# Two re-dated steps in a planned decoder block: VectorE's part of the RNN batches, and the last Strassen product

## The chip, the core and the metric

The kernel runs on one core of a Trainium2 chip. The metric is device microseconds of one launch, from the chip's own clock. Five engines share the work: TensorE (PE in the profile, with its weight loads as PEld), VectorE (DVE), ScalarE (ACT), GpSimd (POOL), and SyncE (SP), which only issues DMAs here.

## The reference, cut to what matters

One decoder block for 512 tokens of width 1024, in float32:

```python
xn   = rms_norm(h, g_mix) * (1 + sc1) + sh1
proj = xn @ w_in + b_in                    # q k v qi ki wi xr yr gate_a gate_b
attn = dsa_attention(q, k, v, qi, ki, wi)  # top-128 keys by an index score, softmax over those
xr   = causal_dwconv(xr)                   # width 4
a    = exp(log_a);  mult = sqrt(-expm1(2 * log_a))
h_r  = scan(a, xr * sigmoid(i) * mult)     # h[s] = a[s] * h[s-1] + u[s]
rnn  = h_r * gelu(yr)
merged = sigmoid(gate_a) * (attn @ w_o_attn) + sigmoid(gate_b) * (rnn @ w_o_rnn)
h    = h + ga1 * (merged @ w_out)
up   = causal_dwconv(xn2 @ w_up)           # width 3, 2 x 2816 columns
h    = h + ga2 * ((silu(gte) * val) @ w_down)
out  = rms_norm(h, g_final)
```

The change touches the order of two things: the scan and the two products around it (`u = xr*i*mult`, `h`, `h*gelu(yr)`), and the end of `act @ w_down`.

## The kernel before, in words

**Arithmetic.** Every float32 product is done as three float32r matmuls (`mm3`): each operand is split into a high part (a copy on ScalarE) and a low part (a subtraction on VectorE, line 470), and PE computes high*high + low*high + high*low. So each weight tile costs VectorE a subtraction before PE can use it. Everything lies in tiles of 128 partitions x 512 columns (`t`, 75 of them); raw weights land in three large buffers (`W`), split weights of projections in six (`w`).

**The planner.** The program is not written in issue order. Each step is recorded with its engine or engines, a cost in us from a formula, what it reads and writes, and optionally a due time; `Plan.order` then simulates the engines and emits the steps in the order in which it would have run them. A step's rank is its due time: the least of `P.fix` (main matmuls, which follow a nominal TensorE clock `clock[0]` that advances 0.227 us for each 512-column matmul), `P.soft`, and what its readers' ranks leave it. An engine takes, among the steps that can start within 0.12 us of the earliest, the one with the lowest rank. A step that needs a new buffer may not start earlier than its rank less a horizon (`P.hor`, normally `HORIZON`). On the chip every engine runs its own list in that order, and a step whose operand is late holds up all that stand behind it on its engine. Most constants in capitals (`ISTEP`, `IW`, `ASTEP`, `AW`, `RB`, `SOON`, `DOT1`, `LATER`, ...) are such due times or lower bounds.

**Stages on PE.** Seven projection tiles accumulate while the first weights arrive; then projection tiles of 24 matmuls each (`proj`); among them the RNN gates, the index scores, attention rows 0 to 3 (`attn_probs`, `attn_out`); the gates `gb`, `ga`; the projections `wr` (of the RNN) and `wa` (of attention); `w_out`; and the FFN.

**The RNN batches.** `rnn_batch` runs for heads 0 to 3 behind tile (yr, 3) and for heads 4 to 7 behind tile (yr, 7). `at(us)` dates a step at `base + us`. All four heads share the dates, so that ScalarE does each function for four tiles in one table phase: square root at `RB[3]` and gelu at `RB[4]`. Before the change VectorE's `u*m` and scan inherit `RB[3]`, and `y*h` inherits `RB[4]`. Behind (yr, 7) come the tiles (q, 1) to (q, 3), whose evacuation (`evac_stack`) ends in a VectorE step on line 475; attention row 0 reads them.

**The FFN's down projection.** `up(n)` makes 44 tiles: `proj`, a convolution (ScalarE, then two steps on line 475), silu and a product for every second one, which gives `acts[f]`, f from 0 to 21. For f up to 15 the down projection is done by Strassen's seven products in two slices (f 0 to 7 and f 8 to 15). `product(m, first, last)` prepares four pairs of operands on VectorE and runs 24 matmuls; `SPREAD` says behind which up tile each runs, `ORDER` which product it is. The remaining f, 16 to 21, are the tail: each output row block of 128 tokens (`ROWS` gives the order 2, 3, 0, 1) and half of the columns takes six `mm3`, then `total` is added, and the final norm and store follow.

Of the kernel before, what the change touches and what calls it, by code (L numbers as in the profile page):

```python
# [14 lines left out]
ALU = mybir.AluOpType  # L15
# [4 lines left out]
TT = S // 128  # L20
D_FF = 2816
FT = D_FF // 128
# [19 lines left out]
SLOTS = {"W": 3, "w": 6, "t": 75, "b": 8}  # L42
SHAPES = {"W": [128, 2048], "w": [128, 1024], "t": [128, 512], "b": [128, 512]}
INFLATE = 1.03
HORIZON = 26
EARLY = 3
PAIRS = 8
ORDER = [[4, 3, 0, 2, 1, 5, 6], [0, 1, 2, 3, 4, 5, 6]]
ROWS = [2, 3, 0, 1]
SLICES = [(0, 4), (4, 8)]  # L50
SPREAD = [[17, 19, 21, 23, 25, 27, 29], [32, 34, 36, 37, 39, 41, 42]]
OUTS = [("wr", (0, 1, 2, 3)), ("wa", (0, 1)), ("wr", (4, 5)), ("wa", (2, 3, 4, 5, 6, 7)), ("wr", (6, 7))]
ADA0 = 28
COLD = 8.0
RBIAS = [14.0, 46.0, 48.0]
WARM = 12
DOT1 = 13.24
SECOND = -23.6
LATER = 13.94
CLOCK = 9.79  # L60
RB = [3.28, 6.04, 7.96, 11.0, 13.85, 0.61]
SOON = [20.91, 19.0, 21.69, 11.19]
ISTEP = {1: 14.0, 2: 38.5, 3: 93.3}
IW = {1: 18, 2: 49.4, 3: 51.9}
ASTEP = {0: 76, 1: 99.0, 2: 126, 3: 145}
AW = [8.6, 6.1, 18.7, 30.4]
BUMP = [0.01, 0.81]


def tile_columns(kind, j):  # L70
# [83 lines left out]
def pass_us(n):  # L154
    return max(0.109, 0.0133 + n / 2400)
# [21 lines left out]
class Plan:  # L177
# [20 lines left out]

    def op(self, engs, reads, writes, emit, func=None, hold=(), n=1, tag="", follow=None):
        o = Op()  # L200
        o.engs, o.emit, o.func = engs, emit, func
        o.n, o.tag = n, tag
        o.shares = self.shares_port(engs, reads, writes, tag)
        o.soft, o.hor, o.after = self.soft, self.hor, self.after
        o.idx, o.fixed, o.succ = len(self.ops), self.fix, []
        deps, bufs = {follow} - {None}, []
        o.weak = set()
        for is_w, vs in ((False, reads), (True, writes)):
            for v in vs:
                if v is None or not isinstance(v, (Buf, View)):  # L210
                    continue
                v = vw(v)
                b = v.buf
                for box, w, p in b.users:
                    if (w or is_w) and overlap(box, v.bx):
                        deps.add(p)
        for is_w, vs in ((False, reads), (True, writes)):
            for v in vs:
                if v is None or not isinstance(v, (Buf, View)):
                    continue  # L220
                v = vw(v)
                v.buf.users.append((v.bx, is_w, o))
                if v.buf not in bufs:
                    bufs.append(v.buf)
        bufs += [b for b in hold if b not in bufs]
        deps.discard(o)
        for b in bufs:
            if b.first is None:
                b.first = o
            elif b.kind in SLOTS and b.first not in deps:  # L230
                o.weak.add(b.first)
        deps.discard(o)
        o.weak -= deps
        deps |= o.weak
        o.deps, o.bufs = deps, bufs
        for p in deps:
            p.succ.append(o)
        self.ops.append(o)
        return o
# [160 lines left out]
def block_kernel(ctx: ExitStack, tc: tile.TileContext, x, cols, wada1, wada2, win0, win, wgate,  # L400
# [10 lines left out]
    P = Plan()  # L411
# [6 lines left out]
    def t2(dt=F32, shape=(128, 512), name="t"):  # L418
        return buf("t", shape, dt, name, 10)

    def bank(reserve=0):
        return buf("b", (128, 512), F32, "ps", reserve)
# [28 lines left out]
    def act(dst, src, func, bias=0.0, scale=1.0, accum=None, hold=()):  # L451
        n = width(src)
        cost = max(0.2, 0.04 + 0.00094 * n) + 0.093 * sum(isinstance(v, (Buf, View)) for v in (bias, scale, accum))
        kw = {}

        def emit(e):
            if isinstance(bias, (Buf, View)) or bias:
                kw["bias"] = real(bias)
            if isinstance(scale, (Buf, View)) or scale != 1.0:
                kw["scale"] = real(scale)  # L460
            if accum is not None:
                kw["accum_out"] = real(accum)
            nc.scalar.activation(real(dst), real(src), func, **kw)  # L463
        P.op({"act": cost}, [src, bias, scale], [dst, accum], emit, func=func.name, hold=hold, n=1 + (accum is not None), tag="act")

    def tt(dst, a, b, op, engs=("dve",)):
        n = max(width(a), width(b))
        c = {"dve": 0.07 + 0.00104 * n, "pool": 0.05 + 0.0026 * n}
        P.op({e: c[e] for e in engs}, [a, b], [dst],
             lambda e: ENG[e].tensor_tensor(real(dst), real(a), real(b), op=op), tag="tt")  # L470
# [66 lines left out]
    def mm3(ps, wh, wl, xh, xl, first, last):  # L537
        mm([(ps, wh, xh, first, False), (ps, wh, xl, False, False), (ps, wl, xh, False, last)])
# [14 lines left out]

    clock = [CLOCK]

    def planned(us):
        P.fix = clock[0]
        clock[0] += us
# [26 lines left out]
    for h in range(2):  # L585
        ps = bank()
# [82 lines left out]
    for kt in range(KT):  # L669
# [26 lines left out]
        cuts = ((0, 2), (2, 4)) if kt == 0 else ((0, 4),)  # L696
        xn.append(modulate(xs, kt, modc[:, 8 + kt:9 + kt], modc[:, kt:kt + 1], cuts))
        for a, b in cuts:
            m = slice(128 * a, 128 * b)
            for n in range(len(G0)):  # L700
                c = slice(n % 4 * 128, n % 4 * 128 + 128)
# [118 lines left out]
    def rnn_batch(js):  # L820
        base = clock[0] + RB[0]

        def at(us):
            P.soft, P.hor = base + us, 1.0
        g = {}
        at(0.0)
        for j in js:
            xc = R[j]
            hi, lo = t2(F32R, name="xch"), t2(F32R, name="xcl")
            split(hi, lo, xc)  # L830
            whi, wlo = wg[j // 2]
            for e, b in ((0, "b_rg"), (1, "b_ig")):
                p = bank(2)
                c = slice(e * 128, (e + 1) * 128)
                mm3(p, whi[:, j % 2, c], wlo[:, j % 2, c], hi, lo, True, True)
                g[j, e] = t2(name="rg")
                act(g[j, e], p, AF.Sigmoid, bias=col(b, j))
            clock[0] += RB[5]
        am = {}
        for j in js:  # L840
            at(RB[1])
            r, u, xc = g[j, 0], g[j, 1], R[j]
            tt(u, u, xc, ALU.mult, ("dve", "pool"))
            t, a, m = t2(name="t"), t2(name="a"), t2(name="m")
            act(t, r, AF.Tanh, scale=sp8[:, j:j + 1])
            at(RB[2])
            act(a, r, AF.Exp, scale=sp8[:, 8 + j:9 + j])
            tt(m, a, a, ALU.mult, ("dve", "pool"))
            stt(m, m, 1.0, t, ALU.add, ALU.mult)
            am[j] = (a, m)  # L850
        for j in js:
            a, m = am[j]
            u = g[j, 1]
            at(RB[3])
            act(m, m, AF.Sqrt)
            tt(u, u, m, ALU.mult, ("dve", "pool"))
            h = t2(name="h")
            vop(1.13, [a, u], [h], lambda h=h, a=a, u=u: nc.vector.tensor_tensor_scan(
                real(h), real(a), real(u), 0.0, op0=ALU.mult, op1=ALU.add))
            y = yg[j]  # L860
            at(RB[4])
            act(y, y, AF.Gelu_apprx_tanh)
            tt(y, y, h, ALU.mult, ("dve", "pool"))
            P.soft, P.hor = None, 20.0
            hi, lo = t2(F32R, name="rh"), t2(F32R, name="rl")
            split(hi, lo, y)
            rnn[j] = (hi, lo)
        P.soft, P.hor = None, HORIZON

# [396 lines left out]
            tt(v, v, ga_b[1][h], ALU.mult)  # L1266
            tt(v, v, back, ALU.add)

    full = slice(0, 512)
    for t in ROWS:  # L1270
        parts, outs = [], []
        c = slice(t * 128, (t + 1) * 128)
        for h in range(2):
            cut = (t, h) == (ROWS[-1], 1)
            for n in [slice(0, 256), slice(256, 512)] if cut else [full]:
                ps = bank()
                for f in range(tail, FT):
                    hi, lo = dsplit[f, h]
                    planned(3 * pass_us(n.stop - n.start))
                    mm3(ps[:, n], asplit[f][0][:, c], asplit[f][1][:, c], hi[:, n], lo[:, n], f == tail, f == FT - 1)  # L1280
                    P.fix = None
                P.soft = clock[0] + 1.0
                v = total[t, h][:, n]
                tt(v, ps[:, n], v, ALU.add)
                o = t2(name="o")
                parts.append(v)
                outs.append((o, n, h))
                P.soft = clock[0] + 2.5
                tt(o[:, n], v, gfin[h][:, n], ALU.mult)
                P.soft = None  # L1290
        P.soft = clock[0] + 1.0
        r = rstd_of(parts)
        for o, n, h in outs:
            w = o[:, n]
            scaled(w, w, r)
            dst = out[t * 128:(t + 1) * 128, h * 512 + n.start:h * 512 + n.stop]
            P.op({"sp": 0.8}, [w], [], lambda e, dst=dst, w=w: nc.sync.dma_start(dst, real(w)))
        P.soft = None
# [100 lines left out]
```

## Time and profile before

| | |
|---|---|
| median of 3 runs | 787.84 us (786.66 to 787.93) |
| the profiled execution | 790.1 us, of which its span 788.3 us |
| PE busy | 768.4 us (97% of the span), 3579 matmuls |
| VectorE busy | 666.9 us (85%) |
| ScalarE busy | 461.4 us (59%) |
| GpSimd busy | 50.5 us (6%) |
| DMA | 126.22 MB, mean 160 GB/s |
| mean granted TensorE clock | 0.992 of full speed |

A matmul's busy time includes its passage through the array, so that consecutive ones overlap in the rows; where PE is never held up the distance from one start to the next is what counts. Granted clock 1.00 is 2.4 GHz, 0.5 is 1.2 GHz.

### The profile page before, as it was taken

Reading aid. Unit: us, or ns where it says so; the run is one execution under the profiler, and the core shown is the slowest. Engines: PE = TensorE matmul, PEld = TensorE weight load, DVE = VectorE, ACT = ScalarE, POOL = GpSimd, SP = SyncE. Lnnn points to the kernel's source line nnn. Section 1 sums busy time; section 2 is a strip of 40 time slices with the busy share of each in tenths; the row PEclk is TensorE's granted clock in tenths of the full one; section 3 lists DMA queues with packets and bytes.
Section 4 is the critical chain, followed back from the end, with each engine's and each line's share of the span. In section 5 each row is a group of like instructions: output and inputs, shape, how many; then the busy total and the mean of one; then the engine's idle time right before and its main releaser. Section 6 shows DMA issues by size and latency. Waiting matters only on the chain.

```text
span 788.3 us, 10204 instructions
## 1 busy us (share of the span) xinstructions
PE 768.4 (97%) x3579; PEld 639.7 (81%) x3579; DVE 666.9 (85%) x1315; ACT 461.4 (59%) x815; POOL 50.5 (6%) x72
## 2 busy tenths in 40 slices
PE   7999999999899999999999999999999999999986
PEld 6888888887788887888789988888888888888865
DVE  6996976999999988869885867897977889997973
ACT  6589935599599779723335643665534454443522
POOL 1000000034021141000000000000000000000000
PEclk9999999999899999999999999999999999999999
DMA  9973132231121351648671343456445544676202
GB/s 342 404 276 111 54 128 85 81 133 54 54 107 55 133 187 55 223 163 312 242 274 39 134 178 116 160 193 209 160 160 199 176 178 155 217 247 201 98 27 81
DMA packets 35411, 126.22 MB, mean 160 GB/s; under 512 B 3944, under 2 KB 6432, under 8 KB 25504
## 3 DMA queue, kind: packets, MB, share of 16 engines
q1 hardware_dynamic: 35360, 125.58, 44.8%
q8 instruction: 28, 0.46, 0.2%
q14 instruction: 23, 0.19, 0.1%
HBM read 121.35 MB, written 5.79 MB: 161 GB/s over the span
## 4 chain that ended last, share of the span: by engine, by line
PE 54%; DVE 24%; DMA 12%; issue 4%; ACT 4%; SPq 0%; POOLq 0%; POOL 0%; DVEq 0%; ACTq 0%
PE ps L534 53%; DMA wd<-in_w_down_dram 7%; DVE dl L470 3%; DMA wr<-in_w_up_dram 3%; DVE wl L470 3%; DVE sum L470 3%; DVE cv L475 2%; DVE wd L470 2%; DVE wa L621 2%; DMA wa<-in_wada_dram 2%; PE ps L546 2%; ACT wh L463 1%; DMA wo<-in_w_out_dram 1%; DVE ahl L470 1%; DVE sc L901 1%
## 5 line engine op out<-in xcount | busy, mean ns | idle before, releaser
L534 PE MATMUL ps<-yl,wh 128*128 128x512 f32 (+1 forms) x376 | 141.7, 377 | 0.1
L534 PE MATMUL ps<-yh,wh 128*128 128x512 f32 (+1 forms) x376 | 141.4, 376 | 0.0
L534 PE MATMUL ps<-yh,wl 128*128 128x512 f32 (+1 forms) x376 | 141.2, 375 | 0.0
L463 ACT ACTIVATE wh<-wr 128x1024 fp32r<-128x1024 f32 (+1 forms) x96 | 97.7, 1019 | 59.6 <-PE ps L534 40.9
L470 DVE TENSOR_TENSOR wl<-wr,wh 128x1024 fp32r<-128x1024 f32 (+1 forms) x96 | 112.9, 1176 | 17.5 <-ACT wh L463 17.1
L534 PE MATMUL ps<-xh,wh 128*128 128x512 f32 x288 | 114.0, 396 | 0.0
L534 PE MATMUL ps<-xh,wl 128*128 128x512 f32 x288 | 113.2, 393 | 0.4 <-DVE wl L470 0.4
L534 PE MATMUL ps<-xl,wh 128*128 128x512 f32 x288 | 113.1, 393 | 0.0
L463 ACT ACTIVATE dh<-wd 128x512 fp32r<-128x512 f32 x68 | 42.5, 630 | 78.0 <-DVE wd L470 69.9
L534 PEld LDWEIGHTS ps<-yl,wh 128*128 128x128 f32 x376 | 70.7, 188 | 13.3 <-DVE yl L470 0.5
L534 PEld LDWEIGHTS ps<-yh,wl 128*128 128x128 f32 x376 | 70.7, 188 | 12.9
L534 PEld LDWEIGHTS ps<-yh,wh 128*128 128x128 f32 x376 | 70.7, 188 | 12.8
L475 DVE SCALAR_TENSOR_TENSOR cv<-ps,ct,cv 128x511 f32<-128x511 f32 x88 | 65.6, 745 | 11.9 <-ACT cv L463 11.2
L534 PE MATMUL ps<-dh,ahl 128*128 128x512 f32 x224 | 71.3, 389 | 0.0
L534 PEld LDWEIGHTS ps<-xh,wl 128*128 128x128 f32 x288 | 54.6, 189 | 12.7 <-DVE wl L470 1.2
L534 PEld LDWEIGHTS ps<-xl,wh 128*128 128x128 f32 x288 | 54.7, 190 | 10.3
L534 PEld LDWEIGHTS ps<-xh,wh 128*128 128x128 f32 x288 | 54.7, 190 | 10.2
L621 DVE SCALAR_TENSOR_TENSOR wa<-wa,crow 128x1024 f32<-128x1024 f32 x48 | 58.5, 1235 | 2.2 <-DMA wa<-in_wada_dram 2.2
L534 PEld LDWEIGHTS ps<-dh,ahl 128*128 128x128 f32 x224 | 42.0, 188 | 8.7
L470 DVE TENSOR_TENSOR dl<-wd,dh 128x512 fp32r<-128x512 f32 x68 | 45.8, 684 | 3.4 <-ACT dh L463 3.1
L463 ACT ACTIVATE cv<-ps,ct 128x512 f32<-128x512 f32 x44 | 33.7, 766 | 17.9 <-PE ps L534 17.9
L534 PE MATMUL ps<-dl,ahl 128*128 128x512 f32 x112 | 43.6, 389 | 0.0
(256 smaller groups left out, 1483.9 us busy)
## 6 DMA issues: line engine op xcount, KB each, us to landing
wa<-in_wada_dram SPq DMA_DIRECT2D x24, 1024.0 KB, 4.8
wd<-in_w_down_dram SPq DMA_DIRECT2D x96, 256.0 KB, 3.4
wr<-in_w_up_dram SPq DMA_DIRECT2D x22, 1024.0 KB, 5.0
wr<-in_win_dram SPq DMA_DIRECT2D x18, 1024.0 KB, 4.8
wr<-in_wo_rnn_dram SPq DMA_DIRECT2D x4, 1024.0 KB, 4.7
wo<-in_w_out_dram SPq DMA_DIRECT2D x4, 1024.0 KB, 4.9
wd<-in_w_down_dram SPq DMA_DIRECT2D x3, 1024.0 KB, 4.9
x<-in_x_dram SPq DMA_DIRECT2D x4, 512.0 KB, 9.6
```

Source lines behind the costliest of these rows:

```text
L463: nc.scalar.activation(real(dst), real(src), func, **kw)
L470: lambda e: ENG[e].tensor_tensor(real(dst), real(a), real(b), op=op), tag="tt")
L475: lambda e: nc.vector.scalar_tensor_tensor(real(dst), real(a), real(s), real(b), op0=op0, op1=op1), tag="stt")
L534: nc.tensor.matmul(real(ps), real(a), real(b), start=st, stop=sp)
L546: nc.tensor.transpose(real(ps[:, i * 128:(i + 1) * 128]), real(s), real(ident))
L621: vop(1.14, [r, crow], [r, dst], lambda: nc.vector.scalar_tensor_tensor(real(r), real(r), 1.0, real(crow), op0=ALU.mult, op1=ALU.mult, acc ...
L901: vop(0.125 + 0.00104 * W, [a, m8], [a], lambda m8=m8: nc.vector.match_replace(real(a), real(m8), real(a), TAKEN))
```

## The change

It does three kinds of thing, and leaves every arithmetic step as it was.

- In `rnn_batch`, VectorE's steps (or GpSimd's, where the planner prefers it) get dates of their own, apart from ScalarE's: `u*m` and the scan at `base + RNNV[batch][0] + RNNV[batch][1] * i` for the i-th head of the batch, `y*h` 3 us after, with a horizon of 20 us.
- The Strassen products are dealt out anew among the up tiles. The last one, which stood behind tile 42, now stands behind tile 43, the last; the one before it behind 42 and not 41. In the tail, the first row block does f 16 to 19 for both column halves first, and then f 20 and 21 for each.
- In the plan, costs on ScalarE, VectorE and GpSimd are multiplied by 1.05 (`SLACK`), the horizon is 41 and not 26 us, and some twenty due times have other values.

```diff
-HORIZON = 26
+HORIZON = 41
-SPREAD = [[17, 19, 21, 23, 25, 27, 29], [32, 34, 36, 37, 39, 41, 42]]
+SPREAD = [[17, 19, 21, 23, 25, 27, 28], [32, 33, 36, 38, 39, 42, 43]]
+SLACK = {"act": 1.05, "dve": 1.05, "pool": 1.05}
-DOT1 = 13.24
-SECOND = -23.6
-LATER = 13.94
-CLOCK = 9.79
-RB = [3.28, 6.04, 7.96, 11.0, 13.85, 0.61]
-SOON = [20.91, 19.0, 21.69, 11.19]
-ISTEP = {1: 14.0, 2: 38.5, 3: 93.3}
-IW = {1: 18, 2: 49.4, 3: 51.9}
-ASTEP = {0: 76, 1: 99.0, 2: 126, 3: 145}
-AW = [8.6, 6.1, 18.7, 30.4]
-BUMP = [0.01, 0.81]
+DOT1 = 14.92
+SECOND = -21.2
+LATER = 8.59
+CLOCK = 9.89
+RB = [3.28, 6.04, 7.96, 11.0, 15.86, 0.61]
+RNNV = [[14.0, 9.1], [24.7, 10.0]]
+SOON = [20.91, 19.0, 22.51, 13.74]
+ISTEP = {1: 14.0, 2: 38.1, 3: 91.6}
+IW = {1: 18, 2: 44.3, 3: 57.2}
+ASTEP = {0: 76, 1: 99.0, 2: 126, 3: 144.9}
+AW = [8.5, 7.3, 18.7, 32.4]
+BUMP = [0.01, 0.74]
...
-        o.engs, o.emit, o.func = engs, emit, func
+        o.engs = {e: c * SLACK.get(e, 1.0) for e, c in engs.items()}
+        o.emit, o.func = emit, func
...
-        for j in js:
+        for i, j in enumerate(js):
             a, m = am[j]
             u = g[j, 1]
             at(RB[3])
             act(m, m, AF.Sqrt)
+            P.soft, P.hor = base + RNNV[js[0] // 4][0] + RNNV[js[0] // 4][1] * i, 20.0
             tt(u, u, m, ALU.mult, ("dve", "pool"))
...
             at(RB[4])
             act(y, y, AF.Gelu_apprx_tanh)
+            P.soft, P.hor = base + RNNV[js[0] // 4][0] + RNNV[js[0] // 4][1] * i + 3.0, 20.0
             tt(y, y, h, ALU.mult, ("dve", "pool"))
...
+    def last(ps, t, h, n, f0, f1):
+        c = slice(t * 128, (t + 1) * 128)
+        for f in range(f0, f1):
+            hi, lo = dsplit[f, h]
+            planned(3 * pass_us(n.stop - n.start))
+            mm3(ps[:, n], asplit[f][0][:, c], asplit[f][1][:, c], hi[:, n], lo[:, n], f == tail, f == FT - 1)
+            P.fix = None
+
+    for i, t in enumerate(ROWS):
+        cuts = [(0, slice(0, 512)), (1, slice(0, 512))]
+        if i == TT - 1:
+            cuts = [(0, slice(0, 512)), (1, slice(0, 256)), (1, slice(256, 512))]
         parts, outs = [], []
+        banks = [bank() for _ in cuts]
+        if i == 0:
+            for ps, (h, n) in zip(banks, cuts):
+                last(ps, t, h, n, tail, FT - 2)
+        for ps, (h, n) in zip(banks, cuts):
+            last(ps, t, h, n, FT - 2 if i == 0 else tail, FT)
+            P.soft = clock[0] + 1.0
...
```

The matmuls, their shapes and their number stay the same, and so do the bytes moved.

## Rows read from the trace of the kernel before

**Rows 1.** The page's second part: PE's busy tenths in 40 slices of 19.7 us.

```profile
PE   7999999999899999999999999999999999999986
```

**Rows 2.** Windows: from:to, us; PE, PEld, DVE, ACT, POOL busy (count); PEclk; DMA.

```profile
206.00:235.00 29.00, 29.00 (x140) 24.22 (x140) 28.04 (x80) 26.56 (x57) 4.47 (x7) 1.00 0.30 110
260.00:300.00 40.00, 39.59 (x188) 32.52 (x187) 37.95 (x93) 31.43 (x61) 15.16 (x19) 1.00 0.44 156
300.00:330.00 30.00, 30.00 (x150) 24.89 (x149) 25.90 (x59) 27.10 (x54) 0.00 (x0) 1.00 0.37 132
...
729.00:743.00 14.00, 14.00 (x63) 11.59 (x62) 13.84 (x24) 7.26 (x12) 0.00 (x0) 1.00 0.34 142
743.00:756.00 13.00, 9.51 (x39) 6.93 (x38) 12.97 (x23) 3.93 (x7) 0.00 (x0) 0.97 0.00 0
```

**Rows 3.** Timeline of PE around 200 us: start, length, instruction, idle before it.

```profile
195.42 0.22 PE L534 MATMUL ps<-kh,q 128*128 128x128 f32 x1
...
197.76 0.30 PE L534 MATMUL ps<-kh,q 128*128 128x128 f32 x1 [2.01 <-DVE q L475]
...
199.33 0.45 PE L534 MATMUL ps<-kh,q 128*128 128x128 f32 x1 [0.93 <-DVE q L475]
...
202.40 0.63 PE L534 MATMUL ps<-xh,wh 128*128 128x512 f32 x1
202.82 0.63 PE L534 MATMUL ps<-xl,wh 128*128 128x512 f32 x1
...
206.04 0.39 PE L534 MATMUL ps<-xh,wh 128*128 128x512 f32 x1
```

**Rows 4.** Timeline of VectorE just before that, like steps merged.

```profile
185.30 3.02 DVE L470 TENSOR_TENSOR rg<-rg,m 128x512 f32<-128x512 f32 x4
188.25 5.23 DVE L858 TENSOR_TENSOR_SCAN h<-a,rg 128x512 f32<-128x512 f32 x4
193.40 2.97 DVE L470 TENSOR_TENSOR yr<-yr,h 128x512 f32<-128x512 f32 x4
...
196.87 3.09 DVE L475 SCALAR_TENSOR_TENSOR q<-ps,ct,q 64x512 fp32r<-64x512 f32 x4
```

**Rows 5.** Timeline of VectorE in the first RNN batch.

```profile
88.37 4.56 DVE L858 TENSOR_TENSOR_SCAN h<-a,rg 128x512 f32<-128x512 f32 x4
```

**Rows 6.** Timeline of GpSimd during the second batch.

```profile
188.47 3.93 POOL L470 TENSOR_TENSOR bm<-bt,mask 128x128 f32<-128x128 f32 x3 [0.69 <-DVE rg L470]
```

**Rows 7.** Timeline of PE in the tail.

```profile
743.08 0.39 PE L534 MATMUL ps<-dh,acth 128*128 128x512 f32 x1
...
749.20 0.39 PE L534 MATMUL ps<-dh,acth 128*128 128x512 f32 x1
...
754.10 0.50 PE L534 MATMUL ps<-dh,acth 128*128 128x512 f32 x1 [2.95 <-ACT acth L463]
...
759.00 0.40 PE L534 MATMUL ps<-dh,actl 128*128 128x512 f32 x1
```

**Rows 8.** Timeline of ScalarE in the tail.

```profile
747.89 0.76 ACT L463 ACTIVATE cv<-ps,ct 128x512 f32<-128x512 f32 x1
```

**Rows 9.** Timeline of VectorE in the tail.

```profile
751.49 1.28 DVE L470 TENSOR_TENSOR sum<-sum,ga 128x512 f32<-128x512 f32 x2
...
753.29 1.29 DVE L470 TENSOR_TENSOR sum<-sum,h 128x512 f32<-128x512 f32 x2
754.50 0.69 DVE L470 TENSOR_TENSOR actl<-cv,acth 128x512 fp32r<-128x512 f32 x1
```

**Rows 10.** Attention's output tiles: duration min/median/max, first and last start, forms.

```profile
L470 DVE TENSOR_TENSOR al<-av,ah x32: 264/280/295, 218.3 to 334.4; 64x128 fp32r<-64x128 f32 x32
...
L534 PE MATMUL ps<-ah,wh x32: 389/389/397, 333.9 to 366.0; 128*128 128x512 f32 x32
```

**Rows 11.** Windows of the conditioning dot products (tile wa): from:to, us, VectorE busy (instructions).

```profile
260.00:300.00 40.00, 8.18 (x12) 1.00 0.44 156
300.00:334.00 34.00, 4.80 (x8) 1.00 0.38 133
```

More of the change, by code (lines that the diff above doesn't have):

```diff
@@ L1267, in block_kernel @@
             tt(v, v, back, ALU.add)
-    full = slice(0, 512)
-    for t in ROWS:
-        parts, outs = [], []
[L1272 to L1290, printed above, removed]
+    def last(ps, t, h, n, f0, f1):
[9 more added lines that the diff above has]
+            cuts = [(0, slice(0, 512)), (1, slice(0, 256)), (1, slice(256, 512))]
+        parts, outs = [], []
+        banks = [bank() for _ in cuts]
[5 more added lines that the diff above has]
+            P.soft = clock[0] + 1.0
+            v = total[t, h][:, n]
+            tt(v, ps[:, n], v, ALU.add)
+            o = t2(name="o")
+            parts.append(v)
+            outs.append((o, n, h))
+            P.soft = clock[0] + 2.5
+            tt(o[:, n], v, gfin[h][:, n], ALU.mult)
+            P.soft = None
         P.soft = clock[0] + 1.0
```

## The prediction, made before the changed kernel was run

> **What bounds the kernel now.** I read the page first, then windows, then the rows of single engines where a window looked odd. The page's busy tenths of PE [rows 1] are all nines except for three dips: the first slice (start), the eleventh, at 197 to 217 us, and the last two, from 749 us. So PE sets the time, and what can be won lies in those dips. At full rate PE starts 63 wide matmuls in 14.00 us (window 729 to 743 of [rows 2]), 0.222 us each; the planner's own figure is 0.227 us for 512 columns and 0.109 us for 128, and I use these two as PE's price of a matmul.
>
> Price of the middle dip. From the first score matmul of attention row 0 at 195.42 to the start at 206.04 [rows 3] pass 10.62 us, in which PE starts ten matmuls of 128 columns and twelve of 512: 10 x 0.109 + 12 x 0.227 = 3.81 us of work. Lost: **6.8 us**. It waits twice for `q` on line 475 (2.01 and 0.93 us), and after that runs wide matmuls 0.42 us apart, at 1.2 GHz, until 206. The reason stands on VectorE [rows 4]: the second RNN batch's `u*m`, scan and `y*h`, twelve steps in a row, 3.02 + 5.23 + 2.97 = 11.2 us, and only then the low parts of `q`.
>
> Price of the dip at the end. From 749.20 to 759.00 [rows 7] pass 9.80 us with 17 wide matmuls, 3.86 us of work. Lost: **5.9 us**, 2.95 of it in one wait for the split of `acts[21]`, and again a stretch at half clock after it. VectorE is busy for 13.84 of 14 and 12.97 of 13 us before [rows 2]: it is the late one. Both dips end on VectorE, though VectorE is free 15% of the span; it is a matter of order.
>
> The profiled execution took 790.1 us (span 788.3, 1.8 around it), 2.3 over the median of the runs, 787.84. Losses are differences, so I take them from the median.
>
> **The change, part by part.**
>
> *RNN dates.* Let C be the plan's clock behind tile (yr, 7). Before, `u*m` and scan of all four heads are due at C + 3.28 + 11.0 = C + 14.3, `y*h` at C + 17.1. Tiles (q, 1) to (q, 3) end 5.45 us apart behind C and are due 20.91 us after that, C + 26 to C + 37, or a little earlier because attention row 0 (76 us behind tile kw, seven tiles before C, so about C + 38) reads them. So all four heads go ahead of every late `q`. After, the scans are due at C + 28, C + 38, C + 48, C + 58: one head goes ahead of or among the `q`, three behind. That takes 3/4 of 11.2 = 8.4 us off VectorE ahead of `q`: its low parts would start at 196.87 - 8.4 = 188.5 and end 3.09 later, at 191.6, before PE comes for them at 195.42 [rows 3, 4]. Bounds: 0 (the steps stay ahead, or something else takes the place) and -6.8 us. I take -5.8, leaving 1.0 for a shorter wait, too short to bring the half clock with it.
>
> Where the 8.4 us goes: into 206 to 330, where VectorE is free for only 0.96, 2.05 and 4.10 us of three windows [rows 2]. What is late next is attention: its last low part starts at 334.4, and the projection that reads it starts at 333.9, without slack [rows 10]. PE would come there 6.8 us sooner, at 327. What gives way: the dot products of the conditioning vectors, 8.18 + 4.80 = 13.0 us from 260 to 334 [rows 11], whose results are wanted only behind the projections, and on PE two tiles of `wr`, 10.9 us, that stand behind the first two of `wa` and need no attention. If neither did, the wait is 334.7 - 327.1 = 7.6 us.
>
> One thing beside it: the four scans took 5.23 us here and 4.56 in the first batch [rows 4, 5]; in the second GpSimd ran `bm` additions meanwhile [rows 6]. By the Trainium skill (SBUF — State Buffer, section "Who interferes with whom") a VectorE step with two inputs in SBUF and a GpSimd step that reads SBUF take turns at a shared port; the 0.67 us agrees with it. By that rule the postponed steps, which meet the `bm` of rows 1 to 3, would be no cheaper there, and the 5.8 would be some 0.7 less.
>
> *Last product and tail.* Before, tile 43 is followed at once by the tail at 743.08 [rows 7]; the tile's ScalarE step ran at 747.89 [rows 8], behind splits that waited for VectorE, and the split of `acts[21]` ended at 754.50 + 0.69 = 755.2 [rows 9]. PE had gone through eleven triples by then. After, tile 43 ends at about 743.1 - 5.4 = 737.6, and behind it stand product 6 (24 x 0.227 = 5.4 us) and eight triples of f 16 to 19 (5.4 us), so that f 20 comes at 748.5 and f 21 at 749.2. The matmuls are the same, and so is VectorE's work ahead of f 21, but product 6's two additions into `total` now come after it, and so can the row block's own `sum` steps, of which two pairs stand among the last operands [rows 9]: 2 x 0.6 + 6 x 0.6 = 4.8 us at 0.6 us a step. If VectorE is the limit, `acts[21]` is there at 755.2 - 4.8 = 750.4: 1.2 us late. If the chain is the limit, 747.89 to 755.2 is 7.3 us and began 4.8 late: 737.6 + 12.1 = 749.7, 0.5 late. If nothing gives way, it is 755.2 still, and the wait is 6.0: no gain. Bounds 0 and -5.9; I take -4.9 (1.0 left).
>
> *Longer durations, wider horizon, other dates.* A step that the plan thinks ready too early is what makes PE wait. Were VectorE full for 40 us ahead of 195 us, 5% would be 2 us, as long as the first wait; over the full 22 us from 729 to 751 it is 1.1 us of 2.95. It helps both dips and is no gain of its own. The horizon lets preparation begin 15 us sooner; PE has nines all through the FFN up to 749 us [rows 1], so nothing can be won there, only lost. The start (`DOT1`, `LATER`, `SECOND`) moves single steps of VectorE about, each some 0.6 us [rows 9]: between -0.6 and +0.6, I take 0. That a new order of everything brings new short waits: 0 to +2, I take +1.0.
>
> Sum: -5.8 - 4.9 + 0 + 1.0 = -9.7; 787.84 - 9.7 = **778.1 us**.
>
> **Rivals.**
>
> *The middle wait moves to attention's reader.* VectorE does the same work, only later, and PE waits up to 7.6 us at the first `wa` tile: the first term is 0, and with the second 787.8 - 4.9 = 783. For it: no slack in [rows 10], VectorE full in [rows 2]. Against: 13.0 us of dot products that can be put off.
>
> *VectorE's backlog at the end stays.* 755.2 as before; only the middle is won: 787.8 - 5.8 + 0.5 = 782.5. For it: both windows full [rows 2].
>
> *Slower: Strassen products too close together.* Behind tiles 27 and 28, 32 and 33, 38 and 39, 42 and 43 two products now have one tile between them; before there were two such places. Two products with two terms on each side want about 2 x 4 x (0.6 + 0.6 + 0.36 + 0.36) = 15.4 us of VectorE (0.6 us a full step, an estimated 0.36 a half-width one), the tile 2.7, the additions into `total` 2.4: 20.5, against 16.3 us of PE. If nothing was prepared ahead, PE waits 4.2 us at each of four places, and half clock behind each adds 1.5: up to 23 us, and past 10.7 us in all, what the two dips give, the kernel is slower: about 793. Against: at the two old places PE has no dip, and the horizon lets more be prepared ahead.
>
> *No effect:* gains and new waits cancel, 787.8.
>
> **Chances.** Forecast 0.56, wait moved 0.13, backlog stays 0.11, slower 0.14, no effect 0.06. The likeliest case's own range runs from both dips gone and a better start (787.8 - 12.7 - 0.6 = 774.5) to little more than half of each with 2 us of new waits (783). With the next two cases whole, and their worse ends, the range is 774 to 787; the rest is left out. A difference under 0.2% (1.6 us) can't be told from no change here: faster 0.80, same 0.06, slower 0.14.
>
> **What the profile after would show.** Right: PE's digits without the eleventh's dip; `q` on line 475 ahead of three of the four scans; granted clock 1.00 around 200 and 756 us; up tile 43 followed by 24 matmuls `dh,ahl` and then the tail, with no wait over 1 us for `acth`. Wrong: a wait of PE for `al` or `ah` near 327 us (first rival), for `acth` near 740 us (second), for `dl` or `ahl` in the FFN (third). The prediction fails most easily in the planner: every step is ordered anew, and the trace of before can't show what that brings.

## The result, and the profile after

The changed kernel takes 777.42 us (median of 4 runs, 777.2 to 779.22), the kernel before 787.88 us (4 runs, 786.66 to 788.89). The ratio is 0.9873, 95% interval 0.9853 to 0.9893: 1.3% faster, 10.5 us by the medians. The forecast was 778.1. The profiled execution took 777.4 us, its span 775.6; that of before was longer than its median, so the two spans differ by 12.7 us.

The page's busy tenths of PE answer to [rows 1]: the eleventh digit and the last but one are nines now, and the engine list has 5.5 us less of busy PE for the same matmuls, since a matmul is longer at half clock, 0.63 us against 0.39 [rows 3].

```profile
PE 762.9 (98%) x3579; PEld 637.0 (82%) x3579; DVE 664.0 (86%) x1304; ACT 459.5 (59%) x814; POOL 68.2 (9%) x83
...
PE   7999999999999999999999999999999999999996
```

The timeline of VectorE around the second RNN batch answers to [rows 4]. Where twelve steps stood in a row ahead of `q`, six low parts of `q` now stand around one scan, and the other three scans follow at 201, 216 and 226 us:

```profile
186.06 1.53 DVE L478 SCALAR_TENSOR_TENSOR q<-ps,ct,q 64x512 fp32r<-64x512 f32 x2
...
188.16 1.21 DVE L862 TENSOR_TENSOR_SCAN h<-a,rg 128x512 f32<-128x512 f32 x1
...
189.86 2.86 DVE L478 SCALAR_TENSOR_TENSOR q<-ps,ct,q 64x512 fp32r<-64x512 f32 x4
...
201.45 1.21 DVE L862 TENSOR_TENSOR_SCAN h<-a,rg 128x512 f32<-128x512 f32 x1
...
203.08 0.68 DVE L473 TENSOR_TENSOR yr<-yr,h 128x512 f32<-128x512 f32 x1
...
225.61 1.22 DVE L862 TENSOR_TENSOR_SCAN h<-a,rg 128x512 f32<-128x512 f32 x1
```

PE's timeline at the same place answers to [rows 3]. Attention row 0's scores start at 195.45, as before, and run through; the granted clock of this stretch is 1.00, where it was at 1.2 GHz for 6.8 us.

```profile
195.45 0.22 PE L537 MATMUL ps<-kh,q 128*128 128x128 f32 x1
...
196.40 0.28 PE L537 MATMUL ps<-kl,q 128*128 128x128 f32 x1
196.51 0.44 PE L537 MATMUL ps<-xh,wh 128*128 128x512 f32 x1
```

The windows (from:to, length, then busy time and count of PE, PEld, DVE, ACT, POOL; PEclk, the granted clock; DMA share and GB/s) answer to [rows 2]. VectorE is as full as it was from 206 to 300 us and fuller behind that, and GpSimd does more than twice as much in the first of them. The last window is the tail:

```profile
206.00:235.00 29.00, 29.00 (x146) 24.37 (x145) 27.92 (x66) 27.66 (x60) 11.98 (x11) 1.00 0.16 53
260.00:300.00 40.00, 40.00 (x197) 33.63 (x196) 38.50 (x98) 34.84 (x70) 15.61 (x19) 1.00 0.33 127
300.00:330.00 30.00, 30.00 (x145) 24.79 (x144) 27.43 (x61) 23.41 (x45) 0.00 (x0) 1.00 0.61 210
...
734.00:747.00 13.00, 12.37 (x51) 8.85 (x50) 13.00 (x24) 5.20 (x10) 0.00 (x0) 1.00 0.00 1
```

In the tail PE no longer waits 2.95 us for `acth` [rows 7]. The only waits that the timeline marks there are two short ones for the low parts of the down weights, `dl`:

```profile
740.89 0.50 PE L537 MATMUL ps<-dl,acth 128*128 128x512 f32 x1 [0.24 <-DVE dl L473]
...
742.70 0.50 PE L537 MATMUL ps<-dl,acth 128*128 128x512 f32 x1 [0.16 <-DVE dl L473]
```

Attention's tiles answer to [rows 10]: its last low part starts at 326.5 and the reader at 326.1, 7.8 us sooner than before, and still without a wait.

```profile
L473 DVE TENSOR_TENSOR al<-av,ah x32: 269/284/296, 210.6 to 326.5; 64x128 fp32r<-64x128 f32 x32
...
L537 PE MATMUL ps<-ah,wh x32: 387/389/398, 326.1 to 358.2; 128*128 128x512 f32 x32
```

**One table for all kernels.** For each trace I took all 3579 starts of matmuls, and from the distance to the next start the price of the matmul (0.109, 0.120, 0.173 or 0.227 us for 128 to 512 columns). What is left is PE's loss, waits and half clock together. The columns are stretches of the span: the start, the first RNN batch, the second with attention row 0, attention's other rows, the output projection, the tail from 730 us. From 520 to 730 us every kernel has -0.3, so PE never waits in the bulk of the FFN; 420 to 520 has 0.7 to 0.9 in all. A trace is one execution; the ratio to the kernel before, timed on the same chip, comes from all runs. The traced execution was the shortest of its kernel's runs in e2, e7 and e10, and the longest in e3, e5, e6 and e12, so the losses in those rows lie at an end of the spread.

| kernel | 0-60 | 60-185 | 185-225 | 225-340 | 340-420 | 730- | ratio (95% interval) |
|---|---|---|---|---|---|---|---|
| before | 6.2 | 0.2 | 6.9 | 2.0 | 0.9 | 5.9 | 1 |
| after | 6.3 | 0.1 | 0.2 | 0.9 | 0.1 | 1.9 | 0.9873 (0.9853 to 0.9893) |
| e1 before + RNN dates | 6.8 | 0.2 | 1.1 | 4.3 | 1.7 | 9.1 | 1.0019 (0.9998 to 1.0040) |
| e2 before + new end | 6.9 | 0.2 | 6.3 | 2.0 | 0.1 | 0.5 | 0.9958 (0.9934 to 0.9981) |
| e5 before + both | 7.0 | 0.2 | 1.1 | 4.6 | 2.1 | 8.2 | 0.9995 (0.9974 to 1.0017) |
| e11 before + longer durations | 7.8 | 7.0 | 5.8 | 1.2 | 0.0 | 0.7 | 1.0040 (1.0016 to 1.0063) |
| e3 after, old RNN dates | 6.9 | 5.7 | 5.7 | 1.0 | -0.1 | 6.9 | 1.0025 (1.0004 to 1.0045) |
| e4 after, old end | 7.2 | 0.1 | 0.2 | 0.9 | 0.1 | 1.7 | 0.9857 (0.9823 to 0.9891) |
| e6 after, old durations | 8.0 | 1.6 | 0.6 | 4.1 | 3.6 | 3.2 | 0.9929 (0.9897 to 0.9961) |
| e7 after, horizon 26 | 6.9 | 0.1 | 0.2 | 0.8 | 0.1 | 0.9 | 0.9867 (0.9820 to 0.9914) |
| e8 after, other dates old | 7.4 | 0.1 | 0.2 | 6.3 | -0.1 | 1.9 | 0.9936 (0.9910 to 0.9961) |
| e9 after, old end, horizon 26 | 5.8 | 0.1 | 0.2 | 0.9 | 1.0 | 4.5 | 0.9893 (0.9861 to 0.9926) |
| e10 after, RNN products on VectorE | 6.1 | 0.1 | 0.2 | 3.4 | 0.0 | 1.4 | 0.9914 (0.9888 to 0.9940) |
| e12 after, attention's dates old | 7.6 | 0.1 | 0.2 | 1.9 | 0.3 | 10.9 | 0.9960 (0.9927 to 0.9992) |

### The profile page after: what moved, and what is told of

Same layout as the page of the kernel before. It is cut to its first block, busy times and chain, and to the rows that moved or that the text cites. A ratio compares the mean times of both kernels' runs of the same rounds, so it can differ in the third digit from the quotient of the medians.

```text
span 775.6 us, 10167 instructions
## 1 busy us (share of the span) xinstructions
PE 762.9 (98%) x3579; PEld 637.0 (82%) x3579; DVE 664.0 (86%) x1304; ACT 459.5 (59%) x814; POOL 68.2 (9%) x83
## 4 chain that ended last, share of the span: by engine, by line
PE 85%; DMA 6%; DVE 6%; issue 2%; ACT 1%; SPq 0%; POOLq 0%; POOL 0%; DVEq 0%
PE ps L537 83%; DMA wd<-in_w_down_dram 4%; DMA wa<-in_wada_dram 2%; PE ps L549 2%; DVE dl L473 1%; DVE wd L473 1%; DVE cv L478 1%; DVE sum L473 1%; DVE wl L473 1%; SPq L452 0%; DVE yf L496 0%; DVE yl L473 0%; DVE cv L473 0%; ACT yf L494 0%; DVE wa L624 0%
## 5 line engine op out<-in xcount | busy, mean ns | idle before, releaser
L537 PE MATMUL ps<-yh,wl 128*128 128x512 f32 (+1 forms) x376 | 141.1, 375 | 0.0
L473 DVE TENSOR_TENSOR wl<-wr,wh 128x1024 fp32r<-128x1024 f32 (+1 forms) x96 | 116.7, 1217 | 21.9 <-ACT wh L466 21.7
L537 PEld LDWEIGHTS ps<-yh,wh 128*128 128x128 f32 x376 | 70.7, 188 | 12.7
L478 DVE SCALAR_TENSOR_TENSOR cv<-ps,ct,cv 128x511 f32<-128x511 f32 (+1 forms) x88 | 65.6, 747 | 4.4 <-ACT cv L466 3.8
L610 POOL TENSOR_TENSOR rstd<-ms,mhalf 128x1 f32<-128x1 f32 x12 | 6.9, 574 | 485.2 <-DVE ms L478 481.1
```

The source lines that it names most:

```text
L478: lambda e: nc.vector.scalar_tensor_tensor(real(dst), real(a), real(s), real(b), op0=op0, op1=op1), tag="stt")
L537: nc.tensor.matmul(real(ps), real(a), real(b), start=st, stop=sp)
L610: lambda: nc.gpsimd.tensor_tensor(real(r), real(ms), real(mhalf), op=ALU.pow), "pool", tag="pow")
```

## The experiments

All compute what the reference does; only the order and the engine of steps differ.

**e1: the RNN dates alone.** Into the kernel before:

```diff
+RNNV = [[14.0, 9.1], [24.7, 10.0]]
+            P.soft, P.hor = base + RNNV[js[0] // 4][0] + RNNV[js[0] // 4][1] * i, 20.0
+            P.soft, P.hor = base + RNNV[js[0] // 4][0] + RNNV[js[0] // 4][1] * i + 3.0, 20.0
```

> The kernel before, with the RNN dates (RNNV) alone. Theory (VectorE's burst ahead of the low parts of q is the whole cause of the middle dip): the low parts of q come ahead of three of the four scans, PE loses under 1 us around 195 us where it lost 6.8, the dip at the end stays at about 5.9; time 787.9 - 6 = 782, between 781 and 783. Rival (the wait moves to the first reader of attention, or the dates work only with the other new dates and the 5% longer durations): PE waits elsewhere between 200 and 340 us, time 785 to 788.

Measured 790.39 us against 790.05. The middle dip goes, 6.9 to 1.1, as the theory had it, and the time stays, above what theory and rival gave. The rival is right that the loss turns up elsewhere, but only in part about where: attention's other rows lose 2.3 us more than before, the output projection 0.8 and the tail, which it did not name, 3.2. PE's waits in this trace (who waited for whom: total, times, longest):

```profile
PE ps L535 <- ACT acth L464: 3.5, 1, 3.5
...
PE ps L535 <- DVE dl L471: 1.9, 3, 0.8
PE ps L535 <- DVE wol L471: 1.4, 1, 1.4
...
PE ps L535 <- DVE ptl L471: 0.8, 2, 0.5
PE ps L535 <- DVE nmax L945: 0.6, 1, 0.6
```

One is long, that for `acth` in the tail (2.95 us before); the others are short: `nmax` and `ptl` in attention's rows, `wol` at the output projection, `dl` in the tail.

**e2: the new end alone.** Into the kernel before, the new `SPREAD` and the new tail loop with `last`.

```diff
-SPREAD = [[17, 19, 21, 23, 25, 27, 29], [32, 34, 36, 37, 39, 41, 42]]
+SPREAD = [[17, 19, 21, 23, 25, 27, 28], [32, 33, 36, 38, 39, 42, 43]]
+            for ps, (h, n) in zip(banks, cuts):
+                last(ps, t, h, n, tail, FT - 2)
...
```

> The kernel before, with the new places of the Strassen products and the new order of the first tail row alone. Theory (more PE work stands behind tile 43, so that its chain is covered): PE loses 1 to 2.5 us in the tail where it lost 5.9, the middle dip stays at about 6.8; time 783.5 to 785. Rival (VectorE's backlog is the limit, and the longer durations or the wider horizon cured it): a wait of over 2 us for acth or for the tail's dl remains, with the half clock behind it, time 786 to 788. Rival (the four places with two products close together): waits for dl or ahl inside the FFN.

Measured 785.98 against 790.05, 0.9958: faster, by some 3 us (1.5 to 5 by the interval). The theory's time holds: as a share of the kernel before, 783.5 to 785 us are 0.994 to 0.996. The tail loses 0.5 where it lost 5.9, the middle still 6.3. The four places with two products close together cost PE nothing.

**e3: the changed kernel with the old RNN dates.**

```diff
-            P.soft, P.hor = base + RNNV[js[0] // 4][0] + RNNV[js[0] // 4][1] * i, 20.0
-            P.soft, P.hor = base + RNNV[js[0] // 4][0] + RNNV[js[0] // 4][1] * i + 3.0, 20.0
```

> The changed kernel, with VectorE's RNN steps dated by ScalarE's phases again. Theory (the dates are the cause): the dip around 190 us is back with a wait for q and a stretch at half clock, 4 to 7 us; time 782 to 784.5. Rival (5% longer durations alone make the plan put attention row 0 later on PE, so that there is no wait): time 777 to 779.

Measured 792.37 us, slower than the kernel before, and far over what either theory gave. The dip at the second batch is back (5.7), and there is one at the first batch, which no trace had shown, and one of 6.9 in the tail, with the new end in place.

**e4: the changed kernel with the old end.** The old `SPREAD` and the old tail loop.

```diff
-SPREAD = [[17, 19, 21, 23, 25, 27, 28], [32, 33, 36, 38, 39, 42, 43]]
+SPREAD = [[17, 19, 21, 23, 25, 27, 29], [32, 34, 36, 37, 39, 41, 42]]
+            for n in [slice(0, 256), slice(256, 512)] if cut else [full]:
+                for f in range(tail, FT):
...
```

> The changed kernel, with the old places of the Strassen products and the old order of the tail. Theory (the end's order is the cause): a wait for acth of 2 to 4 us in the tail, with half clock behind it; time 780 to 782.5. Rival (longer durations and a horizon of 41 us are enough): time 777 to 779, no wait over 1 us in the tail.

Measured 777.53, 0.9857: the same as the changed kernel, within some 3 us by the intervals. The theory falls and the rival holds. The tail loses 1.7 us with the old order, 0.8 of it in a wait for `acth`:

```profile
PE ps L537 <- ACT acth L466: 0.8, 1, 0.8
PE ps L537 <- DVE actl L473: 0.4, 1, 0.4
```

**e5: both cures on the kernel before.** The edits of e1 and e2 together.

```diff
+RNNV = [[14.0, 9.1], [24.7, 10.0]]
+SPREAD = [[17, 19, 21, 23, 25, 27, 28], [32, 33, 36, 38, 39, 42, 43]]
...
```

> The kernel before, with the RNN dates and the new end together, but the plan's old durations, horizon and other dates. First theory (two separate cures, nothing else needed): both dips gone, 0.987 of before. Theory after the first runs (the dates alone trade the middle dip for short waits at attention's rows and at the output projection, the new end cures the tail whatever stands before): the tail loses under 1 us, some 4 us of short waits remain between 200 and 400 us; 0.991 to 0.994 of before.

Measured 789.82 against 789.25. Both theories are wrong about the time and the tail: it loses 8.2 us, so the new end does not cure it whatever stands before. Behind the RNN dates alone PE waits for the down weights' low parts, and for those of the output projection:

```profile
PE ps L535 <- DVE dl L471: 3.7, 4, 2.1
...
PE ps L535 <- DVE wol L471: 1.9, 1, 1.9
```

**e6: the changed kernel with the old durations.**

```diff
-SLACK = {"act": 1.05, "dve": 1.05, "pool": 1.05}
+SLACK = {"act": 1.0, "dve": 1.0, "pool": 1.0}
```

> The changed kernel with the plan's durations as before (factor 1.00). Theory after the first runs (longer durations put attention's and the tail's matmuls later in PE's list, and this is what keeps the postponed RNN work from being waited for): short waits of 3 to 6 us return between 200 and 400 us or in the tail; 0.991 to 0.996 of before. Rival (the durations are no gain of their own, as predicted): within 0.002 of the changed kernel, 0.986 to 0.988.

Measured 783.55 against 789.25, 0.9929: the theory of the longer durations holds in time and place. The profiled execution, 789.1 us, was the longest of the ten, so the sizes in its row are a worst case.

**e7: the changed kernel with the old horizon.**

```diff
-HORIZON = 41
+HORIZON = 26
```

> The changed kernel with the horizon of 26 us. Theory (an earlier start of loads helps only at the output projection, where PE waited 0.8 us before): PE loses 1 to 2 us there; 0.988 to 0.990 of before. Rival (the horizon is what lets VectorE finish the tail's weights early): a wait of over 2 us in the tail, 0.991 to 0.995. Prediction's step (no gain from it): 0.987.

Measured 778.89 against 789.25, 0.9867, and a trace like that of the changed kernel: the prediction's step, no gain from the horizon, holds as far as four runs show it (interval 0.9820 to 0.9914).

**e8: the other dates old.**

```diff
-DOT1 = 14.92
-LATER = 8.59
-SOON = [20.91, 19.0, 22.51, 13.74]
-IW = {1: 18, 2: 44.3, 3: 57.2}
-BUMP = [0.01, 0.74]
+DOT1 = 13.24
+LATER = 13.94
+SOON = [20.91, 19.0, 21.69, 11.19]
+IW = {1: 18, 2: 49.4, 3: 51.9}
+BUMP = [0.01, 0.81]
...
```

> The changed kernel with all the other dates as before (DOT1, SECOND, LATER, CLOCK, SOON, ISTEP, IW, ASTEP, AW, BUMP and the gelu date); RNN dates, new end, longer durations and horizon as changed. Theory (durations and horizon carry it): 0.986 to 0.990 of before. Rival (the other dates are what keeps attention in time behind the postponed RNN work): waits of 3 us or more between 200 and 340 us, 0.991 to 0.996.

All sixteen old values that the change gives a new one are back here. Measured 784.04 against 789.25, 0.9936: the rival holds, with 6.3 us lost from 225 to 340. PE's timeline shows where, and ScalarE's why: between two exponentials of an attention row it loads a table for a gate's sigmoid and loads the old one again, 2 x 1.28 us. In the changed kernel such a pair, at 234.84 and 236.78 us, stands between two groups of four exponentials, and PE waits for neither.

```profile
236.34 0.77 PE L549 MATMUL ps<-ident,l 128*128 128x128 f32 x5 [1.67 <-ACT l L466]
238.52 0.50 PE L537 MATMUL ps<-xh,wh 128*128 128x512 f32 x1 [1.42 <-DVE ptl L473]
```
```profile
231.15 1.28 ACT L466 ACT_TABLE_LOAD   x1
232.45 0.63 ACT L466 ACTIVATE gb<-gb 128x512 f32<-128x512 f32 x1
...
233.50 1.28 ACT L466 ACT_TABLE_LOAD   x1
234.79 0.51 ACT L466 ACTIVATE l<-l,nmax 128x256 f32<-128x256 f32 x1
```

**e9: old end and old horizon together.** The edits of e4 and e7.

```diff
-HORIZON = 41
-SPREAD = [[17, 19, 21, 23, 25, 27, 28], [32, 33, 36, 38, 39, 42, 43]]
+HORIZON = 26
+SPREAD = [[17, 19, 21, 23, 25, 27, 29], [32, 34, 36, 37, 39, 41, 42]]
...
```

> The changed kernel with the old end and the horizon of 26 us together; RNN dates, longer durations and the other dates as changed. Theory (neither the end nor the horizon is needed, each alone having moved nothing): 0.985 to 0.989 of before, PE loses under 2.5 us in the tail. Rival (each stood in for the other): the wait of 3 us or more for acth or dl is back in the tail, with half clock; 0.991 to 0.994.

Measured 780.28 against 788.18, 0.9893 with an interval from 0.9861 to 0.9926, between the two expectations; the tail of the profiled execution loses 4.5 us. Inconclusive: that one stands in for the other in part is possible.

**e10: the RNN's two products on VectorE alone.**

```diff
-            tt(u, u, m, ALU.mult, ("dve", "pool"))
+            tt(u, u, m, ALU.mult)
...
-            tt(y, y, h, ALU.mult, ("dve", "pool"))
+            tt(y, y, h, ALU.mult)
```

> The changed kernel with the RNN's u*m and y*h allowed on VectorE alone, where the plan of the changed kernel gave ten of the sixteen to GpSimd. Theory (the dates win by order; ten steps of 0.6 us more on VectorE cost only what its spare time can't take): 0.986 to 0.990 of before. Rival (it is the ten steps off VectorE that win, in the stretch from 185 to 300 us where it is full): waits of 4 us or more between 185 and 340 us, 0.991 to 0.996. Rival from the shared port: VectorE's weight splits come back from 1266 to 1220 ns and the time is the same or better, 0.983 to 0.987.

Measured 780.22 against 788.18, 0.9914, between theory and first rival, and its interval, from 0.9888, reaches into the theory's range: 225 to 340 us loses 3.4 us where the changed kernel loses 0.9. Ten products on GpSimd are worth 2 to 3 us (2.5 in this stretch of the traces). The third theory falls: the weight splits take 1234 ns and not 1266, and the time is longer.

**e11: the longer durations alone.** Into the kernel before:

```diff
+SLACK = {"act": 1.05, "dve": 1.05, "pool": 1.05}
-        o.engs, o.emit, o.func = engs, emit, func
+        o.engs = {e: c * SLACK.get(e, 1.0) for e, c in engs.items()}
+        o.emit, o.func = emit, func
```

> The kernel before, with the plan's durations 1.05 times as long and nothing else. Theory (a margin alone puts attention row 0 and the tail a little later on PE; the second RNN burst stays ahead of q): the middle dip and the tail lose 2 to 5 us each, 0.993 to 1.000 of before. Rival (the durations are the main thing): both dips under 2 us, 0.987 to 0.990. Rival (margin without new dates makes the plan late everywhere): over 1.002.

Measured 790.58 against 788.18, 1.0040. The third theory has the time, none the place: the tail is cured (0.7), and the first RNN batch loses 7.0 us, as it does in e3 (5.7). VectorE's timeline there, and the wait on PE:

```profile
87.11 2.50 DVE L472 TENSOR_TENSOR rg<-rg,m 128x512 f32<-128x512 f32 x4 [0.37 <-ACT m L465]
89.52 4.57 DVE L860 TENSOR_TENSOR_SCAN h<-a,rg 128x512 f32<-128x512 f32 x4
94.00 2.47 DVE L472 TENSOR_TENSOR yr<-yr,h 128x512 f32<-128x512 f32 x4
96.39 2.35 DVE L472 TENSOR_TENSOR wl<-wr,wh 128x1024 fp32r<-128x1024 f32 x2
```
```profile
97.66 0.80 PE L536 MATMUL ps<-xh,wl 128*128 128x512 f32 x1 [3.92 <-DVE wl L472]
```

Two weight splits stand behind the burst of twelve. In the kernel before one of them stood ahead of it, at 84.13 us, so that PE had a tile more to go on with.

**e12: attention's dates old.**

```diff
-ISTEP = {1: 14.0, 2: 38.1, 3: 91.6}
-IW = {1: 18, 2: 44.3, 3: 57.2}
-ASTEP = {0: 76, 1: 99.0, 2: 126, 3: 144.9}
-AW = [8.5, 7.3, 18.7, 32.4]
+ISTEP = {1: 14.0, 2: 38.5, 3: 93.3}
+IW = {1: 18, 2: 49.4, 3: 51.9}
+ASTEP = {0: 76, 1: 99.0, 2: 126, 3: 145}
+AW = [8.6, 6.1, 18.7, 30.4]
```

> The changed kernel with the dates of scores, top-k and attention (ISTEP, IW, ASTEP, AW) as before. Theory (these four are the ones among the other dates that matter: with all of them old, PE waited 3.1 us for attention row 1 and 2 near 235 us): the wait near 235 us is back, 3 to 5 us with half clock; 0.991 to 0.995 of before. Rival (it was one of the remaining dates): 0.986 to 0.989, no wait over 1 us between 200 and 340 us.

Measured 784.64 against 788.18, 0.9960, with runs from 779.93 to 789.16; the profiled one was the longest. The wait near 235 us is not there, so it is not these four dates that undo it. The loss came by another way, 10.9 us in the tail, where PE waits nine times for `dl`, 5.7 us in all. The last fifteen issues of down weights on SyncE's queue, in the changed kernel and then here:

```profile
698.27 28.36 SPq L452 DMA_DIRECT2D wd<-in_w_down_dram  x15
```
```profile
708.85 28.26 SPq L452 DMA_DIRECT2D wd<-in_w_down_dram  x15
```

They begin 10.6 us later and take as long, while PE at this point is only 2.7 us behind the changed kernel. The queue had fallen behind earlier: its issues of down weights, counted in order, lie 2.8 us behind those of the changed kernel at 525 us, 5.8 at 531 and 9.7 at 611. Why it fell behind there, and whether the four dates or this one execution did it, is open.

## Why the prediction was right, and where its steps were not

**The total.** 778.1 forecast, 777.4 measured. By the table the two spans differ by 6.7 (second batch) + 4.0 (tail) + 1.1 (attention) + 0.8 (output projection) + 0.1 in the remaining stretches = 12.7 us. The forecast's terms were -5.8, -4.9, and +1.0 for new waits. So the middle was priced 0.9 too small, the end 0.9 too large, and in place of new short waits 1.9 us of old ones went. Against these traces the terms are off by 3.0 us in all, and 2.2 of them are taken back because the median of before lay that much under its profiled execution, as the prediction had noted. In which stretch the median run loses less no trace shows, so that the sum comes within 0.7 us is in part luck.

**The middle dip.** Place, price and bound are right: `q`'s low parts come ahead of three of the four scans and all of the 6.8 us goes in the changed kernel; in the other variants with the RNN dates 5.8 or more go. The step "where the 8.4 us goes" is wrong. It said that the conditioning dot products would give way. They do not: from 206 us to the reader of attention they take 15.4 us of VectorE before (2.43 + 8.18 + 4.80 in the windows up to 334 us) and 15.7 after (2.74 + 5.67 + 7.25 up to 326). Nor does VectorE do "the same work, only later", as the first rival has it: once each head has its own date the planner gives ten of the sixteen products to GpSimd, which had none of them before, and seven of the ten are the second batch's (four `u*m` between 180.5 and 193.3 us, three `y*h` at 189.5, 217.3 and 229.2):

```profile
L473 POOL TENSOR_TENSOR rg<-rg,m 128x512 f32<-128x512 f32 x7 | 12.2, 1763 | 80.0 <-PE ps L537 71.1 <-ACT m L466 8.9
...
L473 POOL TENSOR_TENSOR yr<-yr,h 128x512 f32<-128x512 f32 x3 | 4.3, 1438 | 16.0 <-PE ps L537 13.2 <-DVE h L862 2.7
```

The eight products of the second batch took 3.02 + 2.97 = 6.0 us of VectorE [rows 4]; the one that is left, at 203.08, takes 0.68. From 185 us to attention's reader VectorE is busy for 139.6 of 148.9 us before and for 134.6 of 141.1 us after, so of the 7.8 us that the reader comes sooner 5.0 are less work on VectorE and 2.8 less idle time. e10 takes the products back and pays 2 to 3 us. But this is not enough to keep the wait from moving: e1 and e5 give ten products to GpSimd too, six of them of the second batch, and lose the gain. The rows of e1:

```profile
L471 POOL TENSOR_TENSOR rg<-rg,m 128x512 f32<-128x512 f32 x6 | 7.7, 1298 | 11.6 <-ACT m L464 11.6
...
L471 POOL TENSOR_TENSOR yr<-yr,h 128x512 f32<-128x512 f32 x4 | 6.0, 1502 | 86.5 <-DVE h L860 86.5
```

The prediction read `("dve", "pool")`, which stands in both kernels, and did not price it.

**The rival "the wait moves" was not one case among others but the rule.** The prediction gave it 0.13 and one place, attention's reader. In e1 and e5 it happens, spread over attention's rows, the output projection and the tail, and eats the whole gain. It doesn't in the changed kernel because of the parts that the prediction set at nothing: with the old durations (e6) or the other old dates (e8) 4 to 5 us of the 10.5 are lost again (0.9929 and 0.9936 against 0.9873). The step "longer durations help both dips and are no gain of their own" fails in size. Alone they are even a loss (e11): they cure the tail and put a weight split behind the first batch's burst. The RNN dates remove that loss (7.0 us at the first batch in e11, 0.1 in e8, which has both); the durations, with the wider horizon, remove the loss that the RNN dates bring in the tail and at the output projection (8.2 and 2.1 in e5, 1.9 and -0.1 in e8). Neither is worth anything alone. For attention's rows the other dates are needed as well: e8 still loses 6.3 us there. The RNN dates and the durations without the rest were not run.

**The end.** The forecast of the tail was near (-4.9, measured -4.0), its cause was not shown to be the one named. Alone, the new end does what the prediction says (e2). In the changed kernel it is not needed: the old end gives the same time within some 3 us (e4). What cures the tail there without it can be the longer durations, with which alone the tail loses 0.7 (e11). The step that failed is "the matmuls are the same, and so is VectorE's work ahead of f 21": the work is the same, but how far VectorE has got when the tail begins hangs on the whole plan before it. Counted from the tail's first matmul, the last split of `acts` ends after 12.1 us in the kernel before, 9.5 with the old end in the changed kernel, 8.9 with the new one, 12.5 in e5.

**The rest.** The third rival, Strassen products too close together, did not come: no trace shows a loss in the FFN's bulk. No worth of the horizon is seen (e7), as forecast. The start did not move, 6.2 and 6.3 us.

**Open.** Which of the other dates undoes the table loads between attention's exponentials (e8) was not found; the four of e12 alone are not it. Why the runs of the kernel before spread from 784.5 to 795.9 us, and those of e12 over 9 us, is not shown; one trace of e12 has late down weights. Whether the old end and the old horizon together cost something (e9) is not settled.

## What to carry to other kernels

In a kernel whose order is planned as a whole, a wait of the bounding engine is a symptom of which engine is full just before it: removing the wait by putting work off pays only if the readers of what was put off, and of what that work now stands ahead of, still get it in time. Look for the next such reader, and for an engine that can take a share; here that share was worth 2 to 3 us and was not enough by itself. Test the parts alone and each one taken away: here the new RNN dates and the longer durations win nothing alone, yet each is worth several us in company, and a part that helps alone (the new end) is not needed there. A margin on planned durations can push a step behind a burst, as it did alone (e11): look for that step.

## What the runs showed of the hardware that was not expected

A VectorE step that reads two tiles from SBUF can take twice its time while GpSimd works. In the changed kernel GpSimd ran three products from 86.23 to 91.93 us, and in that stretch a weight split and a scan on VectorE took 2.33 and 2.31 us; a few us later, with GpSimd idle, the same two took 1.20 and 1.22:

```profile
86.27 2.33 DVE L473 TENSOR_TENSOR wl<-wr,wh 128x1024 fp32r<-128x1024 f32 x1
88.53 2.31 DVE L862 TENSOR_TENSOR_SCAN h<-a,rg 128x512 f32<-128x512 f32 x1
...
93.03 1.22 DVE L862 TENSOR_TENSOR_SCAN h<-a,rg 128x512 f32<-128x512 f32 x1
94.16 1.20 DVE L473 TENSOR_TENSOR wl<-wr,wh 128x1024 fp32r<-128x1024 f32 x1
```

The prediction had put this at 0.7 us for the four scans of the second batch together; here it is 1.1 us for a single step. By the Trainium skill (SBUF — State Buffer, section "Who interferes with whom") a VectorE instruction with two inputs in SBUF contends with a GpSimd instruction that reads SBUF for the ports that the two share. These rows agree. The exchange was worth it all the same: over the whole kernel the 88 weight splits grew from a mean of 1220 to 1266 ns, 4.0 us in all, of which 1.2 us remain with the products back on VectorE (1234 ns in e10); ten products at some 0.6 us left VectorE for it, and taking them back costs time (e10).
